# Scan of two linear-attention layers: half-width second doubling, one transpose of v, 65-column decays, and the 16x16 solve moved from VectorE to Pool

## The chip, the cores and the metric

The kernel runs on one core of one Trainium2 chip. The metric is the device time of one execution in microseconds; lower is better. A profiled execution is the source of every duration here. Engines are named as in the profile: PE (TensorE), PEld (its weight loads), DVE (VectorE), ACT (ScalarE), POOL (GpSimd), SP (SyncE, which issues most DMAs). L12 is line 12 of the kernel before.

## What is computed

The reference is a stack of a two-layer block (convolution beside a linear-attention scan, then a feed-forward net) and a second block with attention, retention and a mixture of experts. The change touches only the scan of the first block. There are 8 heads of 64 channels, two directions, 256 context tokens and 512 tokens, and two layers:

```python
decay = jnp.exp(-DECAY_SCALE * jax.nn.sigmoid(decay_b0[d] + jnp.tanh(w_lo) @ decay_up[d]))
a = jax.nn.sigmoid(iclr_b0[d] + a_lo @ iclr_up[d])
k_d = k * (1.0 + (a - 1.0) * k_a)
...
def wkv_scan(r, k, v, decay, kk, a, s0, reverse, emit):
    ...
    def step(s, inp):
        r_t, k_t, v_t, w_t, kk_t, b_t = inp          # b = kk * a
        sa = -jnp.einsum("bhvk,bhk->bhv", s, kk_t)
        s = (s * w_t[:, :, None, :] + sa[..., None] * b_t[:, :, None, :]
             + v_t[..., None] * k_t[:, :, None, :])
        y = jnp.einsum("bhvk,bhk->bhv", s, r_t) if emit else None
        return s, y
    s_fin, ys = lax.scan(step, s0, xs, reverse=reverse)
```

## The kernel before

The scan of a layer (`scan`, from L704) is done in 12 steps: four pairs of heads, and for each pair three groups of 256 tokens. A step handles one group forwards (direction 0) and one backwards (direction 1), and a group is four chunks of 64 tokens. In a chunk the recurrence becomes products of 64x64 matrices, among them the inverse of a triangular 64x64 matrix. The stages of a step s are:

- `decay` (L842): two matmuls, tanh, a running sum along each chunk (L863), one or two subtractions (L866, or L870 and L871), three exponentials (L874 to L876).
- `products` (L880): six multiplications per direction that scale k, r and kk by the decays (L887 to L894), matmuls `pg` (L906), and four masked copies of them into `GM` (L910), two per direction. Part of GM is the triangular matrix, called NT.
- `solve` (L674): NT goes to DRAM (`nsc`, L682; for direction 1 a DVE transpose `Nt`, L680, comes first). Its 64 diagonal blocks of 16x16, of both directions, four chunks and two heads, are read back with one block to a partition (`NB`, 64 partitions, one buffer; L684). There 14 rounds of a multiply (L689) and an add (L690), of 14 to 56 elements each and each needing the one before, and one write of the diagonal (L693) invert the blocks. The result goes to DRAM (`xsc`, L694).
- `solved` and `transposed` (L697, L917): four DMAs fetch the inverted blocks into 64x64 form (L702); PE transposes k, b (L925) and v (L932), and ACT copies them out.
- `inverse` (L937): two doublings, from blocks of 16 to 32 and from 32 to 64, each a DVE transpose (L948, one per direction), matmuls `py` (L954), an ACT copy, matmuls `pw` (L963) and a masked DVE copy (L967).
- `chunks` (L974): four rounds, each a chain PE, DVE (`rg`, L992), PE, ACT (L998), PE, DVE (the state M: L1009, or L1011 where there is no state yet). POOL multiplies the old state by the chunk's decay beside it (L1008), and L1009 needs that product.

While step s goes through its chunks, the inverse of step s+1 and the products and solve of step s+2 are written among them (`among`, `to_come`), with the convolution's taps (L533) and other work in the early steps. A scheduler then sets the order in each engine's queue when the program is built; at run time each engine takes its queue in that order, waiting at an instruction whose inputs are not there.

Of the kernel before, what the change touches and what calls it, by code (L numbers as in the profile page):

```python
# [28 lines left out]
CH = 64  # L29
# [22 lines left out]
def shape_constants():  # L52
    p = np.arange(128)[:, None]
    f = np.arange(128)[None, :]
    cf = {}
    cf["ident"] = (p == f).astype(np.float32)
    cf["bones"] = (p // 64 == f // 64).astype(np.float32)
    for d in range(2):
        s, t = p % 64, f % 64
        strict = (s < t) if d == 0 else (s > t)  # L60
        incl = (s <= t) if d == 0 else (s >= t)

        for i in range(2):
# [21 lines left out]

NMASK = 4 * 64
# [42 lines left out]
def tile_two_blocks(ctx: ExitStack, tc: tile.TileContext, I: dict, out: bass.AP, dump=None, stop=None):  # L129
# [508 lines left out]
    def scan_buffers(first_time, RK):  # L638
# [4 lines left out]
        for name, n, cnt in (("GM", 1024, 6), ("KR", 512, 6), ("Z", 512, 4), ("BT", 512, 4), ("XI", 256, 4), ("BK", 512, 4), ("XY", 512, 2),  # L643
                             ("Mn", 128, 4)):
# [29 lines left out]
    def solve(s, T, gs):  # L674
# [29 lines left out]
    def scan(l, S):  # L704
# [13 lines left out]
        S["rs"] = ZZ[2]  # L718
# [123 lines left out]
    def decay(q, l, S, pr, d, g):  # L842
# [9 lines left out]
        tA = wk.tile([128, 4, 256], F32, name="tA", tag="spl", bufs=4)  # L852
        tB = wk.tile([128, 4, 256], F32, name="tB", tag="spl", bufs=4)
        c4 = lambda v: v.rearrange("p (c t) -> p c t", t=CH)
        sa = tA[:, 0:2]
        for i in range(2):
            nc.scalar.activation(tA[:, i], pz[i][:, 0:256], AF.Tanh, scale=0.5,
                                 bias=HB[:, 8 * i + 4 * d + pr:8 * i + 4 * d + pr + 1])
        nc.scalar.activation(sa, sa, AF.Copy, scale=0.5, bias=0.5)
        yield  # L860
        sg, a = tA[:, 0], tA[:, 1]
        cum, oth = tA[:, 2], tA[:, 3]
        nc.vector.tensor_tensor_scan(cum, cst("scan"), sg, 0.0, op0=OP.mult, op1=OP.add)  # L863
        P, Pi, Pp, tmp = tB[:, 0], tB[:, 1], tB[:, 2], tB[:, 3]
        if d == 0:
            nc.vector.tensor_tensor(oth, cum, sg, op=OP.subtract)  # L866
            incl, excl = cum, oth
# [9 lines left out]
        q.update(ts=ts, a=a, P=P, Pi=Pi, Pp=Pp, tmp=tmp)  # L877
        yield

    def products(q, l, S, pr, d, g, KK, get, emit):  # L880

        RK = S["RK"]
        ts, a, P, Pi, Pp, tmp = (q[n] for n in ("ts", "a", "P", "Pi", "Pp", "tmp"))
# [3 lines left out]
        nc.vector.tensor_tensor(KR[:, 0], KK[:, ts], Pp, op=OP.mult)  # L887
        nc.vector.tensor_tensor(tmp, KK[:, ts], a, op=OP.mult)
        nc.vector.tensor_tensor(BK[:, :, 1], c4(tmp), c4(Pi), op=OP.mult)
        nc.scalar.activation(a, a, AF.Identity, scale=vc("k_a", 4 * l + pr), bias=KC[:, pr, 0:1])  # L890
        nc.vector.tensor_tensor(a, a, RK[:, 1, pr % 2, ts], op=OP.mult)
        nc.vector.tensor_tensor(BK[:, :, 0], c4(a), c4(Pi), op=OP.mult)
        if emit:
            nc.vector.tensor_tensor(KR[:, 1], RK[:, 0, pr % 2, ts], P, op=OP.mult)  # L894

        PC = wk.tile([128, 4], F32, name="PC", tag="pc", bufs=6)
        nc.vector.tensor_copy(PC, c4(P)[:, :, 63 if d == 0 else 0])
# [19 lines left out]
    def transposed(q, l, S, pr, d, g, KK, get, emit):  # L917

        BK, VY, t0 = q["BK"], S["VY"], GRP[g][1]
        BT = get("BT").rearrange("p (c a k) -> p c a k", c=4, a=2)  # L920
# [7 lines left out]
        Z = get("Z").rearrange("p (i c v) -> p i c v", i=2, c=4)  # L928
        pv = bank("pg", None, "pv").rearrange("p (i c v) -> p i c v", i=2, c=4)[:, 0]
        for c in range(4):  # L930
            for h in range(2):
                nc.tensor.matmul(pv[HR[h], c], lhsT=VY[HR[h], 0, pr, t0 + CH * c:t0 + CH * c + CH], rhs=ident[HR[h], HR[h]], start=True, stop=True)  # L932
        nc.scalar.activation(Z[:, 0], pv, AF.Copy)
        q.update(Z=Z, BT=BT)
        yield

    def inverse(T, gs):  # L937
# [8 lines left out]
        def first(q, d):  # L946
            a = ("X", "XI") if d == 0 or i else ("XI", "X")
# [17 lines left out]
        def merge(q, d):  # L965
            mk = CM[:, (2 * d + i) * 64:(2 * d + i + 1) * 64]
            nc.vector.copy_predicated(q["XI"], bc(mk), q["p"])  # L967

        for i in range(2):
            for f in (first, left, out_, right, merge):  # L970
                each(f)
                yield

    def chunks(l, S, pr, gs, T, state, emit, final, get):  # L974
# [4 lines left out]
        def chunk(q, d, n):  # L979
# [5 lines left out]
            for h in range(2):  # L985
                nc.tensor.matmul(pr_[HR[h], 0:64], lhsT=GM[HR[h], 0, c, 0], rhs=Z[HR[h], 0, c], start=True, stop=M is None)
# [11 lines left out]
            nc.scalar.activation(Z[:, 1, c], ps_[:, 0:64], AF.Copy)  # L998
            yield
            if not (final and n == 3):  # L1000
                pm = bank("sm", None, "psM")
                for i in range(2):
                    for h in range(2):
                        nc.tensor.matmul(pm[HR[h], 0:64], lhsT=BT[HR[h], c, i], rhs=Z[HR[h], i, c], start=i == 0, stop=i == 1)
# [8 lines left out]
            if emit:  # L1013
# [1168 lines left out]
```

## Time and profile before

| | |
|---|---|
| median of 3 runs | 4024.76 us (4021.48 to 4025.88) |
| profiled execution, its time | 4035.13 us |
| its span | 4033.3 us |
| PE / DVE / ACT / POOL busy | 94% / 68% / 42% / 8% |
| mean granted TensorE clock | 0.961 |
| scan of the first layer | about 293 to 701 us |
| scan of the second layer | about 1530 to 1895 us |

Busy times are unions of an engine's instructions. A matmul's end is modelled, so a high share of PE is not PE at its limit. Rows of a timeline give the start and the time of an instruction, or of several alike in a row; "[0.82 <-PE pg L906]" is idle time of the engine just before it and what ended it.

### The profile page before, as it was taken

The numbers are of one execution on the slowest core, as the hardware profiler recorded it, in microseconds if no ns is written. First come the engines' busy times: TensorE is split into PE (matmuls) and PEld (weight loads), VectorE is DVE, ScalarE is ACT, GpSimd is POOL, SyncE is SP. The second block draws the span as 40 slices with busy tenths as digits, with TensorE's granted clock in tenths as the row PEclk, the third lists the DMA queues.
The fourth block names the chain that finished last, engine by engine and source line by source line (L and its number), as shares of the span: only waits on it lengthen the run. The fifth ranks groups of instructions, "written<-read, shape, count | busy, mean of one in ns | idle before, by whom it ended". The sixth has DMA issues, their size and how long they took to land. (4 is left out here: it accounts for less than half of the span.)

```text
span 4033.3 us, 69782 instructions
## 1 busy us (share of the span) xinstructions
PE 3787.4 (94%) x27963; PEld 2847.6 (71%) x27963; DVE 2757.5 (68%) x5535; ACT 1707.5 (42%) x2552; POOL 330.9 (8%) x301
## 2 busy tenths in 40 slices
PE   6998999999999998899999998997999999999997
PEld 4786777788888786776787786675565777764443
DVE  4778875753433778876745455657877899987776
ACT  3234352321212334442322244544655676666565
POOL 0000111000000000110000000001101122122111
PEclk8999999999999998899999998997999999999999
DMA  6122323332422221123545421035979899998996
GB/s 206 44 79 67 113 65 95 124 126 84 126 79 90 96 71 27 32 42 107 164 138 165 108 81 42 1 117 186 348 289 347 304 360 369 369 353 327 373 370 241
DMA packets 353980, 677.87 MB, mean 168 GB/s; under 512 B 118760, under 2 KB 230195, under 8 KB 323539
## 3 DMA queue, kind: packets, MB, share of 16 engines
q1 hardware_dynamic: 343024, 636.89, 45.1%
q0 software_dynamic: 9376, 34.63, 3.4%
q8 instruction: 221, 3.62, 0.4%
q10 hardware_dynamic: 1250, 1.85, 0.1%
q14 instruction: 109, 0.89, 0.1%
HBM read 635.39 MB, written 37.90 MB: 167 GB/s over the span
## 5 line engine op out<-in xcount | busy, mean ns | idle before, releaser
L431 ACT ACTIVATE wh<-wst 128x1024 fp32r<-128x1024 f32 (+2 forms) x222 | 222.8, 1004 | 988.9 <-PE pc L441 519.9
L1795 DVE TENSOR_TENSOR ml<-E,mh 128x2048 fp32r<-128x2048 f32 x236 | 536.1, 2286 | 92.0 <-PE pu L1843 44.3
L1794 ACT ACTIVATE mh<-E 128x2048 fp32r<-128x2048 f32 x236 | 447.7, 1916 | 187.6 <-PE pu L1843 147.5
L441 PE MATMUL px<-Hh,wl 128*128 128x512 f32 (+2 forms) x1216 | 485.9, 400 | 15.6 <-DVE wl L432 15.5
L441 PE MATMUL px<-Hh,wh 128*128 128x512 f32 (+3 forms) x1216 | 485.3, 401 | 13.6 <-ACT wh L431 7.1
L441 PE MATMUL px<-Hl,wh 128*128 128x512 f32 (+3 forms) x1216 | 484.7, 399 | 1.0 <-DVE Hl L419 1.0
L432 DVE TENSOR_TENSOR wl<-wst,wh 128x1024 fp32r<-128x1024 f32 (+2 forms) x222 | 255.4, 1152 | 270.5 <-ACT wh L431 268.2
L1843 PE MATMUL pu<-ml,ch 128*64 128x512 f32 (+2 forms) x968 | 273.0, 399 | 21.1 <-DVE ml L1795 20.9
L1843 PE MATMUL pu<-mh,ch 128*128 128x512 f32 (+1 forms) x968 | 280.2, 404 | 6.9 <-DVE ch L1831 4.2
L441 PEld LDWEIGHTS px<-Hh,wl 128*128 128x128 f32 (+1 forms) x1216 | 231.0, 190 | 74.7 <-DVE wl L432 20.9
L441 PEld LDWEIGHTS px<-Hh,wh 128*128 128x128 f32 (+1 forms) x1216 | 231.4, 191 | 72.9 <-ACT wh L431 9.7
L441 PEld LDWEIGHTS px<-Hl,wh 128*128 128x128 f32 (+1 forms) x1216 | 231.2, 190 | 57.0 <-DVE Hl L419 5.0
L533 DVE SCALAR_TENSOR_TENSOR acc<-ZC,VT,acc 128x272 f32<-128x272 f32 (+2 forms) x600 | 253.6, 479 | 2.6 <-ACT acc L528 2.5
L1843 PEld LDWEIGHTS pu<-mh,ch 128*128 128x128 f32 (+1 forms) x968 | 172.4, 185 | 86.8 <-issue 25.4
L1795 DVE TENSOR_TENSOR ml<-st,mh 128x2048 fp32r<-128x2048 f32 x86 | 196.0, 2286 | 42.8 <-PE pu L1843 24.5
L1843 PEld LDWEIGHTS pu<-ml,ch 128*64 128x64 f32 (+2 forms) x968 | 149.8, 159 | 90.7 <-DVE ml L1795 32.3
L441 PE MATMUL pc<-Hh,wh 128*128 128x256 f32 x672 | 192.9, 288 | 0.9 <-ACT Hh L418 0.9
L441 PE MATMUL pc<-Hl,wh 128*128 128x256 f32 x672 | 191.7, 285 | 0.5 <-DVE Hl L419 0.5
L441 PE MATMUL pc<-Hh,wl 128*128 128x256 f32 (+1 forms) x672 | 190.4, 284 | 0.1
L1794 ACT ACTIVATE mh<-st 128x2048 fp32r<-128x2048 f32 x86 | 163.2, 1917 | 55.4 <-PE pu L1843 31.7
L315 DVE SCALAR_TENSOR_TENSOR as<-adt,CS,as 128x512 f32<-128x512 f32 x224 | 161.3, 747 | 33.8 <-DMA adt<-in_w_ada_dram 19.4
L1099 DVE SCALAR_TENSOR_TENSOR XT<-px,MOD,XT 128x512 f32<-128x512 f32 x66 | 49.5, 750 | 188.9 <-PE px L441 188.6
(596 smaller groups left out, 7949.8 us busy)
## 6 DMA issues: line engine op xcount, KB each, us to landing
E<-in_w_mlp_dram SPq DMA_DIRECT2D x288, 1024.0 KB
st<-in_w_mlp_dram SPq DMA_DIRECT2D x94, 1024.0 KB
wst<-in_w_in_dram SPq DMA_DIRECT2D x29, 1024.0 KB
adt<-in_ada_w_dram SPq DMA_DIRECT2D x96, 256.0 KB
adt<-in_w_ada_dram SPq DMA_DIRECT2D x96, 256.0 KB
wst<-in_ffn_wg_dram SPq DMA_DIRECT2D x22, 1024.0 KB
wst<-in_ffn_wu_dram SPq DMA_DIRECT2D x22, 1024.0 KB
adaw<-in_ada_w_dram SPq DMA_DIRECT2D x16, 1024.0 KB
```

What stands on the lines that cost most here:

```text
L315: nc.vector.scalar_tensor_tensor(acc[s], t, c, acc[s], op0=OP.mult, op1=OP.add)
L431: nc.scalar.activation(wh, t[:, :, c0:c0 + n], AF.Copy)
L432: nc.vector.tensor_tensor(wl, t[:, :, c0:c0 + n], f32(wh), op=OP.subtract)
L441: nc.tensor.matmul(p[0:m, 0:n], lhsT=wa[:, k, 0:m], rhs=ha[:, k, a:a + n], start=k == 0 and first, stop=k == nk - 1 and last)
L533: nc.vector.scalar_tensor_tensor(o, z[:, j + a:j + a + n], cw(j), o, op0=OP.mult, op1=OP.add)
L1099: nc.vector.scalar_tensor_tensor(o, src, gate, o, op0=OP.mult, op1=OP.add)
L1794: nc.scalar.activation(wh, t, AF.Copy)
L1795: nc.vector.tensor_tensor(wl, t, f32(wh), op=OP.subtract)
L1843: nc.tensor.matmul(p[0:xa.shape[2]], lhsT=xa[:, kt], rhs=w[part][:, c:c + 512], start=kt == 0 and j == 0, stop=last and j == len(parts) - 1)
```

## The change

Four things change in the scan.

1. The 14 rounds and the diagonal write of `solve` are issued on POOL instead of DVE. The DMAs around them stay where they were.
2. The second doubling works on the 32 columns that it needs: transposes of 32 of each 64 columns, matmuls with 32 moving columns, and a plain copy of 32 rows per head, on DVE for one head and on ACT for the other, where a masked copy of everything was.
3. v is transposed once for each pair of heads and group and kept in a ring of four buffers (`V`), not once per direction; `Z` is split into `V` and `SA`.
4. The running sum has 65 columns per chunk, the first a zero that POOL writes (two memsets of 128x4 per step), so that the inclusive and exclusive sums are two views of it: one subtraction falls away in either direction, two exponentials take the place of three, and the multiplications of k and b by the inverse decay become one of 512 columns.

```diff
-            nc.vector.tensor_tensor(t, NB[:, 0:k, k:k + 1].to_broadcast(sh), NB[:, k:k + 1, k + 1:16].to_broadcast(sh), op=OP.mult)
-            nc.vector.tensor_tensor(NB[:, 0:k, k + 1:16], NB[:, 0:k, k + 1:16], t, op=OP.add)
+            nc.gpsimd.tensor_tensor(t, NB[:, 0:k, k:k + 1].to_broadcast(sh), NB[:, k:k + 1, k + 1:16].to_broadcast(sh), op=OP.mult)
+            nc.gpsimd.tensor_tensor(NB[:, 0:k, k + 1:16], NB[:, 0:k, k + 1:16], t, op=OP.add)
...
-        nc.vector.tensor_scalar(NB.rearrange("p a b -> p (a b)")[:, 0:256:17], ones[0:64, 0:16], 1.0, None, op0=OP.mult)
+        nc.gpsimd.tensor_scalar(NB.rearrange("p a b -> p (a b)")[:, 0:256:17], ones[0:64, 0:16], 1.0, None, op0=OP.mult)
...
+        nc.gpsimd.memset(full[:, 0, :, 0:1], 0.0)
...
-        nc.vector.tensor_tensor_scan(cum, cst("scan"), sg, 0.0, op0=OP.mult, op1=OP.add)
-        P, Pi, Pp, tmp = tB[:, 0], tB[:, 1], tB[:, 2], tB[:, 3]
-        if d == 0:
-            nc.vector.tensor_tensor(oth, cum, sg, op=OP.subtract)
...
+        nc.vector.tensor_tensor_scan(tA[:, 520:780], cst("scan"), tA[:, 0:260], 0.0, op0=OP.mult, op1=OP.add)
+        if d:
+            rest = c4(tB[:, 516:776])
+            nc.vector.tensor_tensor(rest, sums[:, :, 64:65].to_broadcast([128, 4, 65]), sums, op=OP.subtract)
...
-        nc.scalar.activation(P, incl, AF.Exp, scale=-CDEC)
-        nc.scalar.activation(Pi, incl, AF.Exp, scale=CDEC)
-        nc.scalar.activation(Pp, excl, AF.Exp, scale=-CDEC)
...
+        nc.scalar.activation(E, sums, AF.Exp, scale=-CDEC)
+        nc.scalar.activation(Pi, sums[:, :, incl], AF.Exp, scale=CDEC)
...
-        nc.vector.tensor_tensor(BK[:, :, 1], c4(tmp), c4(Pi), op=OP.mult)
...
-        nc.vector.tensor_tensor(BK[:, :, 0], c4(a), c4(Pi), op=OP.mult)
...
+        nc.vector.tensor_tensor(BK.rearrange("p c a t -> p a c t"), sa,
+                                Pi[:, None].to_broadcast([128, 2, 4, CH]), op=OP.mult)
...
+        if (pr, g) not in Vs:
+            Vs[pr, g] = get("V").rearrange("p (c v) -> p c v", c=4)
...
+        def first2(q, d):
+            nc.vector.transpose(q["X"][:, :, half(d)], q["XI"][:, :, half(d)])
...
+                    nc.tensor.matmul(q["p"][HR[h], c], lhsT=q["NT"][HR[h], c], rhs=q["X"][HR[h], c, half(d)], start=True, stop=True)
...
+        def merge2(q, d):
+            for h in range(2):
+                rows = slice(64 * h + 32 * d, 64 * h + 32 * d + 32)
+                o = q["XI"][rows, :, half(1 - d)]
+                if h:
+                    nc.scalar.activation(o, q["p"][rows], AF.Copy)
+                else:
+                    nc.vector.tensor_copy(o, q["p"][rows])
```

The scheduler orders the queues anew. First place: DVE in the second layer's scan, where the masked copies into GM and the transpose `Nt` of the eighth step's solve stand beside the first transposes (of `X` and `XI`, here under the name of their buffer, XT) of the seventh step's inverse. Before:

```order
L910 TENSOR_TENSOR scanbuf_14686<-pg,CB 128x512
L992 TENSOR_SCALAR rg<-psR 128x64
L910 TENSOR_TENSOR scanbuf_14686<-pg,CB 128x512
L992 TENSOR_SCALAR rg<-psR 128x64
L910 TENSOR_TENSOR scanbuf_14686<-pg,CB 128x512 x2
L680 STREAM_TRANSPOSE Nt<-scanbuf_14686 128x256
L543 SCALAR_TENSOR_TENSOR ZC_13447<-cmean,acc 128x512
L1009 SCALAR_TENSOR_TENSOR XT<-psM,PC,XT 128x64 x2
L549 COPY CVC<-cvar 128x8
L948 STREAM_TRANSPOSE XT<-XT 128x256
```

The same place now:

```order
L1027 TENSOR_SCALAR rg<-psR 128x64
L908 TENSOR_TENSOR scanbuf_14542<-pg,CB 128x512
L1027 TENSOR_SCALAR rg<-psR 128x64
L908 TENSOR_TENSOR scanbuf_14542<-pg,CB 128x512
L948 STREAM_TRANSPOSE XT<-XT 128x256
L908 TENSOR_TENSOR scanbuf_14542<-pg,CB 128x512
L948 STREAM_TRANSPOSE XT<-XT 128x256
L908 TENSOR_TENSOR scanbuf_14542<-pg,CB 128x512
L680 STREAM_TRANSPOSE Nt<-scanbuf_14542 128x256
```

`Nt` of the next step stood ahead of the inverse's first transpose; it now stands behind it.

Second place: DVE one step on. Before, the products stand ahead of the inverse's transposes:

```order
L892 TENSOR_TENSOR XT<-tA,tB 128x4x64
L690 TENSOR_TENSOR NB<-NB,nbt 64x14
L1011 TENSOR_SCALAR XT<-psM,PC 128x64 x2
L992 TENSOR_SCALAR rg<-psR 128x64 x2
L910 TENSOR_TENSOR scanbuf_14686<-pg,CB 128x512
L338 RECIPROCAL rcn<-rcn 128x8
L910 TENSOR_TENSOR scanbuf_14686<-pg,CB 128x512 x3
L1050 TENSOR_TENSOR VY<-spread,VY 128x512
L948 STREAM_TRANSPOSE XT<-XT 128x256
L680 STREAM_TRANSPOSE Nt<-scanbuf_14686 128x256
```

Now (L887 to L892 are products, L908 the copies into GM; four more rows, then `Nt`):

```order
L948 STREAM_TRANSPOSE XT<-XT 128x256
L887 TENSOR_TENSOR tA<-zz_14544,tA 128x4x64
L888 TENSOR_TENSOR tA<-tA,RK 128x4x64
L887 TENSOR_TENSOR tA<-zz_14544,tA 128x4x64
L948 STREAM_TRANSPOSE XT<-XT 128x256
L889 TENSOR_TENSOR XT<-tA,tB 128x2x4x64
L888 TENSOR_TENSOR tA<-tA,RK 128x4x64
L892 TENSOR_TENSOR scanbuf_14543<-RK,tB 128x256
L889 TENSOR_TENSOR XT<-tA,tB 128x2x4x64
L895 COPY PC<-tB 128x4
L1046 TENSOR_SCALAR XT<-psM,PC 128x64 x2
L908 TENSOR_TENSOR scanbuf_14542<-pg,CB 128x512
```

Seven of the products have moved behind the first transpose, so that they too lie between it and `Nt`.

Third place: the end of a solve, the one of the second step of the first layer, on DVE before (other work lies between its operations), and the same solve on POOL now, with what follows it there (L1043 is the decay of the state, L1008 before).

```order
L689 TENSOR_TENSOR nbt<-NB 64x26
L690 TENSOR_TENSOR NB<-NB,nbt 64x13x2
L1009 SCALAR_TENSOR_TENSOR XT<-psM,PC,XT 128x64
L689 TENSOR_TENSOR nbt<-NB 64x14
L1009 SCALAR_TENSOR_TENSOR XT<-psM,PC,XT 128x64
L690 TENSOR_TENSOR NB<-NB,nbt 64x14
L533 SCALAR_TENSOR_TENSOR acc<-ZC_479,VT,acc 128x272 x2
L992 TENSOR_SCALAR rg<-psR 128x64 x2
L533 SCALAR_TENSOR_TENSOR acc<-ZC_479,VT,acc 128x239
```

```order
L689 TENSOR_TENSOR nbt<-NB 64x26
L690 TENSOR_TENSOR NB<-NB,nbt 64x13x2
L689 TENSOR_TENSOR nbt<-NB 64x14
L690 TENSOR_TENSOR NB<-NB,nbt 64x14
L1043 TENSOR_SCALAR XT<-XT,PC 128x64 x6
L689 TENSOR_TENSOR nbt<-NB 64x14
L693 TENSOR_SCALAR NB<-ones 64x16
```

The solve stands in POOL's queue in one piece, and the decays of the state stand behind it.

## Rows read from the trace of the kernel before

**Rows 1.** Windows of both scans: PE, PEld, DVE, ACT, POOL busy us (instructions).
```profile
293.00:701.00 408.00, 367.11 (x6915) 292.36 (x6914) 317.99 (x1141) 162.66 (x411) 43.92 (x87) 0.97 0.31 83
1530.00:1895.00 365.00, 325.15 (x6311) 265.01 (x6312) 275.80 (x1027) 156.66 (x406) 47.05 (x84) 0.92 0.20 45
```
**Rows 2.** Line L694, the DMA behind each solve: first and last start, by scan.
```profile
L694 SPq DMA_DIRECT2D xsc<-NB x12: 574/575/596, 330.9 to 661.7; - x12
...
L694 SPq DMA_DIRECT2D xsc<-NB x12: 574/574/590, 1566.8 to 1856.6; - x12
```
**Rows 3.** Groups by line, whole run: count, busy us, mean ns of one, idle before.
```profile
L690 DVE TENSOR_TENSOR NB<-NB,nbt 64x14 f32<-64x14 f32 (+6 forms) x336 | 62.7, 187 | 2.3
L689 DVE TENSOR_TENSOR nbt<-NB 64x14 f32<-64x14 f32 (+6 forms) x336 | 62.6, 186 | 8.7 <-DMA NB<-nsc 6.5
L948 DVE STREAM_TRANSPOSE XT<-XT 128x256 f32<-128x256 f32 x96 | 40.6, 432 | 7.8 <-DMA XT<-xsc 7.5
L932 PE MATMUL pv<-CF,VY 64*64 64x64 f32 x768 | 28.3, 221 | 0.2 <-issue 0.2
L954 PE MATMUL py<-XT,scanbuf 64*64 64x64 f32 x1536 | 69.0, 229 | 11.2 <-DVE XT L948 8.7 <-DMA XT<-xsc 1.8
L963 PE MATMUL pw<-XT 64*64 64x64 f32 x1536 | 62.1, 226 | 1.0 <-ACT XT L957 0.4
```
**Rows 4.** Timeline of SP around one solve of the second layer: start us, us.
```profile
1752.71 1.23 SPq L682 DMA_DIRECT2D nsc<-Nt  x2
1755.56 0.59 SPq L684 DMA_DIRECT2D NB<-nsc  x1
1767.60 0.57 SPq L694 DMA_DIRECT2D xsc<-NB  x1
1770.16 2.94 SPq L702 DMA_DIRECT2D XT<-xsc  x4
```
**Rows 5.** Timeline of DVE in the same stretch.
```profile
1749.71 0.69 DVE L910 TENSOR_TENSOR scanbuf<-pg,CB 128x512 f32<-128x512 f32 x1 [0.18 <-PE pg L906]
1750.72 0.69 DVE L910 TENSOR_TENSOR scanbuf<-pg,CB 128x512 f32<-128x512 f32 x1 [0.32 <-PE pg L906]
...
1752.28 0.40 DVE L680 STREAM_TRANSPOSE Nt<-scanbuf 128x256 f32<-128x256 f32 x1
...
1759.38 0.16 DVE L689 TENSOR_TENSOR nbt<-NB 64x14 f32<-64x14 f32 x1
...
1763.35 0.21 DVE L689 TENSOR_TENSOR nbt<-NB 64x56 f32<-64x56 f32 x1
1763.59 0.21 DVE L690 TENSOR_TENSOR NB<-NB,nbt 64x56 f32<-64x56 f32 x1
...
1773.58 0.45 DVE L948 STREAM_TRANSPOSE XT<-XT 128x256 f32<-128x256 f32 x1
```
**Rows 6.** Tile NB: ns min/median/max, first and last start us.
```profile
L689 DVE TENSOR_TENSOR nbt<-NB x336: 135/189/245, 314.7 to 1856.2; 64x14 f32<-64x14 f32 x24, 64x36 f32<-64x36 f32 x24, 64x50 f32<-64x50 f32 x24, 64x56 f32<-64x56 f32 x24
...
L684 SPq DMA_DIRECT2D NB<-nsc x24: 573/592/598, 312.0 to 1845.8; - x24
```
**Rows 7.** POOL's arithmetic: the state's decay by line, and line L1756's times.
```profile
L1008 POOL TENSOR_SCALAR XT<-XT,PC 128x64 f32<-128x64 f32 x160 | 85.0, 542 | 895.9 <-DVE XT L1011 373.9 <-DVE XT L1009 342.9 <-DVE nbt L689 92.9
...
L1756 POOL TENSOR_TENSOR hr<-hr,AS x8: 1255/1405/3039, 2752.8 to 2769.2; 128x512 f32<-128x512 f32 x8
```
**Rows 8.** Timeline of DVE, then POOL: a state and its decays.
```profile
1844.25 0.47 DVE L1009 SCALAR_TENSOR_TENSOR XT<-psM,PC,XT 128x64 f32<-128x64 f32 x2
...
1844.62 0.85 POOL L1008 TENSOR_SCALAR XT<-XT,PC 128x64 f32<-128x64 f32 x2 [11.37 <-DVE XT L1009]
```
**Rows 9.** Timeline of DVE, then POOL: a row of products beside one decay.
```profile
1690.62 0.41 DVE L887 TENSOR_TENSOR scanbuf<-zz,tB 128x256 f32<-128x256 f32 x1
...
1693.30 0.41 DVE L891 TENSOR_TENSOR tA<-tA,RK 128x256 f32<-128x256 f32 x1
...
1690.79 3.23 POOL L1008 TENSOR_SCALAR XT<-XT,PC 128x64 f32<-128x64 f32 x1 [1.11 <-DVE XT L1009]
```

More of the change, by code (lines that the diff above doesn't have):

```diff
@@ L851, in decay @@
         yield
[L852 to L855, printed above, removed]
+        tA = wk.tile([128, 1024], F32, name="tA", tag="spl", bufs=4)
+        tB = wk.tile([128, 1024], F32, name="tB", tag="spl", bufs=4)
+        c4 = lambda v: v.rearrange("p (c t) -> p c t", c=4)
+        full, sums = tA[:, 0:520].rearrange("p (i c t) -> p i c t", i=2, c=4), c4(tA[:, 520:780])
@@ L927, in transposed @@
         yield
[L928 to L934, printed above, removed]
+        if (pr, g) not in Vs:
+            Vs[pr, g] = get("V").rearrange("p (c v) -> p c v", c=4)
+            pv = bank("pg", None, "pv").rearrange("p (i c v) -> p i c v", i=2, c=4)[:, 0]
+            for c in range(4):
+                for h in range(2):
+                    nc.tensor.matmul(pv[HR[h], c], lhsT=VY[HR[h], 0, pr, t0 + CH * c:t0 + CH * c + CH], rhs=ident[HR[h], HR[h]], start=True, stop=True)
+            nc.scalar.activation(Vs[pr, g], pv, AF.Copy)
+        q.update(Z=(Vs[pr, g], SA), BT=BT)
         yield
@@ L946, in first @@
         def first(q, d):
-            a = ("X", "XI") if d == 0 or i else ("XI", "X")
+            a = ("X", "XI") if d == 0 else ("XI", "X")
             nc.vector.transpose(q[a[0]], q[a[1]])
@@ L965, in merge, with left2, out2, right2 @@
         def merge(q, d):
-            mk = CM[:, (2 * d + i) * 64:(2 * d + i + 1) * 64]
+            mk = CM[:, d * 64:(d + 1) * 64]
             nc.vector.copy_predicated(q["XI"], bc(mk), q["p"])
[L969 to L972, printed above, removed]
+        for f in (first, left, out_, right, merge):
+            each(f)
+            yield
+        half = lambda d: slice(32 * d, 32 * d + 32)
+        c32 = lambda v: v[:, 0:128].rearrange("p (c t) -> p c t", c=4)
+        def first2(q, d):
+            nc.vector.transpose(q["X"][:, :, half(d)], q["XI"][:, :, half(d)])
+        def left2(q, d):
+            q["p"] = c32(bank("iv", None, "py"))
+            for c in range(4):
+                for h in range(2):
+                    nc.tensor.matmul(q["p"][HR[h], c], lhsT=q["NT"][HR[h], c], rhs=q["X"][HR[h], c, half(d)], start=True, stop=True)
+        def out2(q, d):
+            nc.scalar.activation(q["Y"][:, :, 0:32], q["p"], AF.Copy)
+        def right2(q, d):
+            q["p"] = c32(bank("iv", None, "pw"))
+            for c in range(4):
+                for h in range(2):
+                    nc.tensor.matmul(q["p"][64 * h + 32 * d:64 * h + 32 * d + 32, c], lhsT=q["Y"][HR[h], c, 0:32], rhs=q["XI"][HR[h], c, half(1 - d)],
+                                     start=True, stop=True)
+        def merge2(q, d):
+            for h in range(2):
+                rows = slice(64 * h + 32 * d, 64 * h + 32 * d + 32)
[4 more added lines that the diff above has]
+                    nc.vector.tensor_copy(o, q["p"][rows])
+        for f in (first2, left2, out2, right2, merge2):
+            each(f)
+            yield
     def chunks(l, S, pr, gs, T, state, emit, final, get):
@@ L985, in chunk @@
             for h in range(2):
-                nc.tensor.matmul(pr_[HR[h], 0:64], lhsT=GM[HR[h], 0, c, 0], rhs=Z[HR[h], 0, c], start=True, stop=M is None)
+                nc.tensor.matmul(pr_[HR[h], 0:64], lhsT=GM[HR[h], 0, c, 0], rhs=Z[0][HR[h], c], start=True, stop=M is None)
             for h in range(2):
@@ L1003, in chunk @@
                     for h in range(2):
-                        nc.tensor.matmul(pm[HR[h], 0:64], lhsT=BT[HR[h], c, i], rhs=Z[HR[h], i, c], start=i == 0, stop=i == 1)
+                        nc.tensor.matmul(pm[HR[h], 0:64], lhsT=BT[HR[h], c, i], rhs=Z[i][HR[h], c], start=i == 0, stop=i == 1)
                 yield
@@ L1018, in chunk @@
                     for h in range(2):
-                        nc.tensor.matmul(po[HR[h], c], lhsT=Z[HR[h], i, c], rhs=GM[HR[h], i, c, 1], start=M is None and i == 0, stop=i == 1)
+                        nc.tensor.matmul(po[HR[h], c], lhsT=Z[i][HR[h], c], rhs=GM[HR[h], i, c, 1], start=M is None and i == 0, stop=i == 1)
         for n in range(4):
```

47 lines of the change are left out of this document (22 added, 25 removed).

## The prediction

> **What bounds the kernel now.** I read first the windows of the two scans, since the change touches nothing else [rows 1]. They hold 773 us of the span. DVE is busy for 318 of 408 us and 276 of 365; PE shows 90%, but with modelled ends. Next I looked for the pace. The DMA that follows each solve is issued at 330.9 for the first of twelve steps and at 661.7 for the last, in the second layer at 1566.8 and 1856.6 [rows 2]: 22 periods in 620.6 us, 28.2 us each. What fills a period? The SP and DVE timelines of one step [rows 4, 5] show a loop with two hops through DRAM:
>
> - `Nt` ends at 1752.68, and NB's read is issued at 1755.56, so 2.9 us;
> - NB's read to the first multiply takes 2.7 us where DVE is free: 312.0 to 314.7 [rows 6];
> - the solve;
> - the DMA behind it at 1767.60, the read back at 1770.16, the first transpose of the inverse at 1773.58: 6.0 us.
>
> So from `Nt` to the transpose of the same step there are 11.6 us of DMA and handover plus the solve. I use 11.5. On DVE the solve alone runs at 0.24 us per operation (1763.35 to 1763.59 [rows 5]), 7.0 us for 29; with other work between its operations it takes from 8 (1759.38 to 1767.60 here [rows 4, 5]) to 16 us (314.7 to 330.9 in the first step [rows 2, 6]). Is the loop closed, that is, does `Nt` of the next step wait for the transpose? In the order before, often not: the first two places show `Nt` ahead of the transpose, or just behind it with all products done. Transposes then found their data there: the waits of L948 for the DMA come to 7.5 us in the whole run [rows 3]. DVE's own queue, solves included, sets the period before, more than the loop does.
>
> **The change, part by part.**
>
> The solve. 29 operations per step leave DVE: 62.7 + 62.6 us [rows 3] and 24 diagonal writes of about 0.16 (an estimate, between the smallest multiply, 0.135, and the mean, 0.186 [rows 3, 6]), 129 us of DVE. On POOL the trace shows no such operation. The nearest row is the state's decay, 64 columns: two of them in 0.85 us, so 0.44 for one and 0.41 from start to start, and POOL started it some 0.09 us after the end of the first state (which takes some 0.28 of the pair's 0.47 from 1844.25, an estimate, since the two overlap; the decay starts at 1844.62) [rows 8]. The solve has 14 to 56 columns, 40 on average, but two tensor inputs, and each operation waits for the one before. I take 0.41 + 0.09 = 0.50 us, 14.5 us per solve, because that row is nearest in size. Lower bound: DVE's pace, 0.24, 7 us. Upper bound: the decay's mean with its waits, 0.542 [rows 7], and 0.09, 18.3 us.
>
> The page "GPSIMD Engine Reference" of the Trainium skill (section 3.1) gives 4497 ns for a two-input operation of 2048 columns there against 2293 on DVE, and advises against elementwise work on that engine. With the 1255 ns at 512 columns in this trace [rows 7] an estimate from that page is 0.17 us fixed and 2.1 ns a column, so 0.26 us for 40 columns; with the handover the solve would take 10 us, and the sum below would give about no change. No run here shows it.
>
> The order. The scheduler has put the transpose earlier: in the first two places it now stands ahead of `Nt` of the next step. This closes the loop. Between the first transpose and `Nt` lie, in the first place, two transposes of 0.43, two masked copies of 0.69 and `Nt`, 2.6 us; in the second seven products, four copies and more, some 9 us; where a new pair of heads begins some 15. Counted so over all 22 pairs of steps in the new order, the mean is 6.3 us. Instructions overlap by some 0.07 us each, which takes 1 us off; the four masked copies wait for PE (1749.71 and 1750.72 are 1.01 apart, against 0.69 for one [rows 5]), which adds 1.2. I take 6.5.
>
> The new period is then 6.5 + 11.5 + 14.5 = 32.5 us against 28.2, 4.3 more. Two of the 22 periods, the first of each layer, aren't ruled by it, because there the next `Nt` still stands ahead: 20 x 4.3 = 86 us. DVE's own work can't fill it: 594 us busy in both scans [rows 1] less the relief is some 430 of 773.
>
> The other edits, beside the loop. One subtraction less per direction and step, 48 of 0.41 as for a product of the same 256 columns [rows 9], 20 us of DVE; one exponential less on ACT; two multiplications of 0.41 joined into one of 512 columns, which I take at 0.69 by the masked copy [rows 5], 0.13 x 48 = 6 us. Half the transposes of v: 14 of 28.3 us of PE and half their ACT copies. The second doubling is half of 69.0 + 62.1 us of PE with half the columns: between 0 and 33 us. Its 48 transposes of 0.43 [rows 3] and as many masked copies, which I take at the same, get narrower, at most to half, up to 21 us of DVE, and 48 short copies go to ACT. None of it but the decays and products stands between a transpose and `Nt`, so I give the path 6 us for all of it, at the ends of the scans where no loop covers it. If the loop did not rule, DVE's 129 + 20 + 6 + some 15 = 170 us would count, and a good part of that would be gained.
>
> New waits. The state's decay (L1043) now stands behind a whole solve on POOL (third place). Who waits is the state's update on DVE, and behind it the next chunk. That update stands in DVE's queue near the transpose, which waits 6.0 us longer than the solve's end, so it costs nothing as long as the transpose is the later one; without that cover, up to a solve per step. The 48 memsets of four columns are bounded by 0.44 each, 21 us of POOL, behind the same solves and ahead of a running sum on DVE that has the same cover: 0. The two reloads of RK per new pair go through POOL's queue too, behind a solve: 0 to 4 us each time, at four places, 0 to 16 us, and I take 0, since products of the new pair stand behind the transpose that is later still. SP's queue keeps its DMAs; its issue of the solve's result waits for POOL in place of DVE, and what is queued behind it are the reads that need it.
>
> Sum: +86 - 6 = +80 us. The profiled execution took 4035.13 us, 10.4 over the median, so 4115 for it and 4105 on the median's scale.
>
> **The rivals.**
>
> Fast POOL. If an operation takes 0.32 us, between DVE's pace and mine, the solve is 9.3 us and the period 27.3: 20 x -0.9 - 6, about -25, and down to -70 at DVE's pace. The time would be 4000 (3955 to 4015). For it: the smallest columns are 14, and 1255 ns for 512 columns leave little fixed cost. Against: 0.41 for the nearest row, and the dependence. It decides from 0.35 us per operation downward.
>
> No change: 0.36 us, a solve of 10.5, period 28.5. With the 6 us off, 4025.
>
> POOL starved by DVE. A decay took 3.23 us, from 1690.79, while DVE ran nine products from two buffers without a gap (the first begun at 1690.62, the last at 1693.30), and ended 0.3 us after the last of them [rows 9]; the decay's mean is 0.1 over its 0.44 [rows 7, 8]. With 28 operations in a row such waits add up: at 0.3 us each 0.8 per operation, a solve of 23 us in the ten dense steps with taps and 18 in the others. That gives 10 x 12.8 + 10 x 7.8 - 6 = +200: 4225. Against: DVE idles while it waits for the transpose, and then POOL is free. I take the half of it as likely as the whole. The page "SBUF — State Buffer" of the Trainium skill (Who interferes with whom) has this as a rule: a DVE instruction with two SBUF inputs and a GpSimd instruction that reads SBUF share a read interface, and the second to come is blocked. The trace agrees, by the 3.23 us.
>
> The loop doesn't rule. If chunks or PE are later than the transpose anyway, the 170 us of DVE count by a third or so and the kernel gains 50 us: 3975. For it: PE's 90%. Against: before, the transposes hardly waited, and the solve's way through DRAM is fixed.
>
> **How the numbers follow.** Forecast (POOL at 0.42 to 0.6 us): 0.52, 4060 to 4160. Starved: 0.15, 4160 to 4225. No change: 0.08. Fast POOL: 0.17. Loop doesn't rule: 0.08. So slower by over 0.2% (8 us, about what can be told from no change here) 0.67, same 0.08, faster 0.25. The range leaves out half of the starved case and the lower part of the two fast ones: 3985 to 4190.
>
> **What would show it.** Right: the time from the first multiply to the last add on POOL at 13 to 18 us; solve-to-solve periods of 31 to 34 us; DVE idle of some 5 to 10 us per step in front of the first transpose with the DMA as releaser, where it was 7.5 us in all; DVE busy in the scans down by 150 us or more without gain. Wrong: solves on POOL under 10.5 us, periods under 28; or L948 waiting for nothing, and DVE or PE full. Starved: operations on POOL of a microsecond and more beside taps and products. The most exposed number is the 0.50 us per operation: each 0.1 us is 2.9 us per step and 58 us in all.

## The result, and the profile after

The changed kernel takes 4130.26 us (median of 4, 4120.13 to 4138.77) against 4024.61 (4021.48 to 4025.88): 1.0254 times as long, 95% interval 1.0235 to 1.0273. Between the profiled executions the span went from 4033.3 to 4118.3 us, 85 more; the one before lies 10 us above its kernel's median and the one after 10 below. The profile shows what turned up between two solves. First the scans, which now end at about 740 and 1985 us (columns as in [rows 1]):

```profile
293.00:740.00 447.00, 367.28 (x6634) 294.15 (x6634) 268.88 (x737) 154.50 (x396) 152.83 (x455) 0.90 0.27 74
1560.00:1985.00 425.00, 326.88 (x6180) 268.74 (x6179) 237.48 (x657) 151.63 (x399) 148.16 (x456) 0.88 0.17 38
```

PE's busy time is that of [rows 1] within 2 us, in stretches that are 39 and 60 us longer. DVE is busy 506 us where it was 594. The granted clock of the scans is 0.90 and 0.88, where it was 0.97 and 0.92. The DMA behind each solve, by scan (as in [rows 2]):

```profile
L694 SPq DMA_DIRECT2D xsc<-NB x12: 574/575/590, 327.3 to 704.4; - x12
...
L694 SPq DMA_DIRECT2D xsc<-NB x12: 574/574/590, 1602.7 to 1946.4; - x12
```

The 22 periods sum to 720.8 us, 32.8 each, against 28.2: 100 us more. The groups by line that answer [rows 3, 7] (L1043 is the state's decay, L908 the masked copies into GM, which waited 16.0 us before):

```profile
L948 DVE STREAM_TRANSPOSE XT<-XT 128x256 f32<-128x256 f32 x48 | 21.1, 442 | 135.2 <-DMA XT<-xsc 135.2
L908 DVE TENSOR_TENSOR scanbuf<-pg,CB 128x512 f32<-128x512 f32 x80 | 54.9, 687 | 41.5 <-PE pg L904 41.0
L954 PE MATMUL py<-XT,scanbuf 64*64 64x64 f32 x768 | 50.6, 298 | 103.7 <-DVE XT L948 103.7
L963 PE MATMUL pw<-XT 64*64 64x64 f32 x768 | 35.2, 247 | 0.3 <-ACT XT L957 0.3
L689 POOL TENSOR_TENSOR nbt<-NB 64x14 f32<-64x14 f32 (+6 forms) x336 | 108.5, 323 | 90.8 <-DMA NB<-nsc 67.6
L690 POOL TENSOR_TENSOR NB<-NB,nbt 64x14 f32<-64x14 f32 (+6 forms) x336 | 106.5, 317 | 23.6
L1043 POOL TENSOR_SCALAR XT<-XT,PC 128x64 f32<-128x64 f32 x160 | 74.1, 473 | 336.1 <-DVE XT L1044 308.0 <-DVE XT L1046 27.8
```

DVE now waits 135.2 us in front of L948 for the blocks that come back from DRAM; it waited 7.8. Behind it PE waits 103.7 us at L954 for that transpose, where it was 11.2. One period shows the whole loop. SP, POOL and DVE in the second layer (start us, us; POOL's first and last rows of a solve):

```profile
1713.04 0.57 SPq L694 DMA_DIRECT2D xsc<-NB  x1
1715.55 2.60 SPq L702 DMA_DIRECT2D XT<-xsc  x4
...
1727.82 0.59 SPq L684 DMA_DIRECT2D NB<-nsc  x1
1743.94 0.57 SPq L694 DMA_DIRECT2D xsc<-NB  x1
```
```profile
1731.14 0.21 POOL L689 TENSOR_TENSOR nbt<-NB 64x14 f32<-64x14 f32 x1
...
1743.70 0.22 POOL L690 TENSOR_TENSOR NB<-NB,nbt 64x14 f32<-64x14 f32 x1
```
```profile
1718.55 0.45 DVE L948 STREAM_TRANSPOSE XT<-XT 128x256 f32<-128x256 f32 x1 [6.32 <-DMA XT<-xsc]
...
1722.77 0.69 DVE L908 TENSOR_TENSOR scanbuf<-pg,CB 128x512 f32<-128x512 f32 x1 [1.43 <-PE pg L904]
...
1724.39 0.44 DVE L680 STREAM_TRANSPOSE Nt<-scanbuf 128x256 f32<-128x256 f32 x1
...
1750.72 0.45 DVE L948 STREAM_TRANSPOSE XT<-XT 128x256 f32<-128x256 f32 x1 [6.73 <-DMA XT<-xsc]
```

Read it round: transpose at 1718.55, `Nt` ends at 1724.83 (6.3), NB's read is issued at 1727.82 (3.0), the first multiply starts at 1731.14 (3.3), the last addition ends at 1743.92 (12.8), and the next transpose starts at 1750.72 (6.8). Each waits for the one before (the first multiply here also for two decays of the state, which POOL starts at 1730.32); 32.2 us in all.

PE's part in the stretch from the transpose to `Nt` (columns as in [rows 1]):

```profile
1713.00:1719.00 6.00, 0.00 (x0) 0.00 (x0) 0.45 (x2) 0.00 (x0) 0.92 (x5) 0.84 0.24 44
1719.00:1722.00 3.00, 2.95 (x44) 2.95 (x46) 2.34 (x7) 0.77 (x2) 0.00 (x0) 0.50 0.28 65
```

PE does nothing for 6 us while it waits for the transpose. When it starts, its granted clock is 0.50, the lower of TensorE's two levels (1.2 of 2.4 GHz), and the matmuls done at it are those of the inverse and `pg`, on which the masked copies and `Nt` wait. By the clock records of the trace, 18 of the 20 steps behind the first of each layer have such a piece between transpose and `Nt`, 4.6 us a step on the mean; in the kernel before it is one step of 20. L954's mean is 298 ns, where it was 229 [rows 3].

### The profile page after: what moved, and what is told of

It reads as the page before. It is cut to its first block, busy times and chain, and to the rows that moved or that the text cites. A ratio compares the mean times of both kernels' runs of the same rounds, so it can differ in the third digit from the quotient of the medians.

```text
span 4118.3 us, 69005 instructions
## 1 busy us (share of the span) xinstructions
PE 3776.6 (92%) x27579; PEld 2843.4 (69%) x27579; DVE 2660.8 (65%) x4743; ACT 1693.9 (41%) x2529; POOL 540.9 (13%) x1045
## 5 line engine op out<-in xcount | busy, mean ns | idle before, releaser
L441 PE MATMUL px<-Hh,wl 128*128 128x512 f32 (+2 forms) x1216 | 485.3, 399 | 14.5 <-DVE wl L432 14.5
L533 DVE SCALAR_TENSOR_TENSOR acc<-ZC,VT,acc 128x272 f32<-128x272 f32 (+2 forms) x600 | 251.0, 480 | 2.6 <-ACT acc L528 2.5
L1957 POOL DMA_INDIRECT out_dram<-XT,idx x34 | 116.7, 3433 | 513.0 <-DVE XT L1955 284.6
```

Of the source, the lines that this page charges most:

```text
L441: nc.tensor.matmul(p[0:m, 0:n], lhsT=wa[:, k, 0:m], rhs=ha[:, k, a:a + n], start=k == 0 and first, stop=k == nk - 1 and last)
L533: nc.vector.scalar_tensor_tensor(o, z[:, j + a:j + a + n], cw(j), o, op0=OP.mult, op1=OP.add)
L1957: nc.gpsimd.indirect_dma_start(out=ov, out_offset=bass.IndirectOffsetOnAxis(ap=idx[:, 0:1], axis=0), in_=y, in_offset=None, compute_op=OP.add)
```

## The experiments

**Which of the four edits.** The solve back on DVE (its multiply, its addition, shown here, and its diagonal write), the other three edits kept:

```diff
-            nc.gpsimd.tensor_tensor(NB[:, 0:k, k + 1:16], NB[:, 0:k, k + 1:16], t, op=OP.add)
+            nc.vector.tensor_tensor(NB[:, 0:k, k + 1:16], NB[:, 0:k, k + 1:16], t, op=OP.add)
```

> The changed kernel with its solve put back on DVE; the three other edits stay. The scheduler then puts Nt of the next step ahead of the transpose again in most steps. Theory (loop through the solve closed by the new order, with the solve on Pool as its cause): faster than the kernel before by 20 to 45 us (3980 to 4005), the wait of the first transposes for their DMA back under 10 us in all (135 us in the changed kernel). Rival (the other edits are at fault: memsets of Pool ahead of the running sums, ACT copies, narrow copies): slower than before by 50 us or more.

4001.82 us, ratio 0.9956 (0.9935 to 0.9977). And the reverse, the kernel before with nothing but these three instructions on POOL:

> The kernel before with its solve on Pool and nothing else. Its order, too, has the transpose ahead of Nt, with 0.7 to 1.3 us per step more between them than the changed kernel. Theory: the loop closes as in the changed kernel, periods of 33 to 34 us, 4120 to 4170, so slower than before by as much as the whole change or somewhat more. Rival (other edits at fault): within 20 us of the kernel before.

4162.3 us, ratio 1.035 (1.0324 to 1.0376). First the kernel with the solve on DVE, the DMA behind each solve by scan and the group of L948:

```profile
L694 SPq DMA_DIRECT2D xsc<-NB x12: 574/575/590, 323.5 to 649.6; - x12
...
L694 SPq DMA_DIRECT2D xsc<-NB x12: 574/575/590, 1546.2 to 1828.7; - x12
```
```profile
L948 DVE STREAM_TRANSPOSE XT<-XT 128x256 f32<-128x256 f32 x48 | 20.9, 435 | 8.7 <-DMA XT<-xsc 8.7
```

Then the same of the kernel with nothing but the solve on POOL:

```profile
L694 SPq DMA_DIRECT2D xsc<-NB x12: 574/575/581, 322.6 to 715.0; - x12
...
L694 SPq DMA_DIRECT2D xsc<-NB x12: 574/574/575, 1619.2 to 1981.9; - x12
```
```profile
L948 DVE STREAM_TRANSPOSE XT<-XT 128x256 f32<-128x256 f32 x96 | 40.5, 433 | 147.2 <-DMA XT<-xsc 146.5 <-issue 0.4
```

Periods of 29.6 and 25.7 us without the move, 35.7 and 33.0 with it alone, and the wait comes and goes with it. In how many steps is the loop closed? Of the 20 steps behind the first of each layer, `Nt` of the next step ends behind the first transpose in 10 in the kernel before, in all 20 in the changed kernel and with the move alone, and in 5 with the solve back on DVE. The solve on POOL is the whole loss; the three other edits gain 20 us where it is on DVE (4022 to 4002) and 32 where it is on POOL (4162 to 4130; 35, if each is set against the runs of the kernel before beside it). The kernel with all but the move is the fastest of the study, faster than both.

**Does the period follow the solve?** Rounds 8 to 14 left out:

```diff
-        for k in range(1, 15):
+        for k in range(1, 8):
```

> The changed kernel with rounds 1 to 7 of the solve's 14, so 14 operations on Pool in place of 28; the rest of the inversion is left out. Theory: the solve takes about 6 us in place of 11.7, and each us is one of the period in about 20 of 22 periods: -116 us, less some 25 us for a little more work between transpose and Nt in its order: 4030 to 4060, DVE's wait before the first transposes still there. Rival (Pool and DVE contend for SBUF, and the time is lost in slower instructions of DVE, not in the loop): half of the loss comes back at most, so 4070 to 4085, with the wait before the transposes little changed per step and DVE instructions shorter.

4029.93 us, ratio 1.0026 (1.0011 to 1.0041). The other way, with a second copy of the multiply:

```diff
             nc.gpsimd.tensor_tensor(t, NB[:, 0:k, k:k + 1].to_broadcast(sh), NB[:, k:k + 1, k + 1:16].to_broadcast(sh), op=OP.mult)
+            nc.gpsimd.tensor_tensor(t, NB[:, 0:k, k:k + 1].to_broadcast(sh), NB[:, k:k + 1, k + 1:16].to_broadcast(sh), op=OP.mult)
```

> The changed kernel with each multiply of the solve issued twice, 42 operations per step on Pool; results are the same. Theory: the solve grows by 14 x 0.4 = 5.6 us, 112 us over 20 periods; its order has 1.2 us less per step between transpose and Nt, so 85 to 110 us slower than the changed kernel: 4205 to 4250. If the loop does not rule the period, well under that: under 4170.

4216.37 us, ratio 1.0481 (1.0454 to 1.0508). The solve took 6.3, 11.7 and 16.8 us in the three kernels (a mean over the steps, first multiply to last addition), the period 29.0, 32.8 and 36.5. So 0.7 us of period for each microsecond of solve on both sides: the loop rules, and a part of what the solve gains is lost again by the way from the transpose to `Nt`, which got longer when the solve was cut and shorter when it was stretched.

**Is it POOL's speed or the order?** On POOL the solve is no slower than it was on DVE among other work: 11.9 and 11.6 us in the two scans, against 13.4 and 11.8. So the loss should be in what stands between transpose and `Nt`. The writing order changed, so that products and `Nt` of step s+2 are emitted ahead of the inverse of s+1:

```diff
-            if s + 1 < 12:
-                works.append(inverse_of(s + 1))
-                for _ in range(3):
-                    yield next(works[0])
             if s + 2 < 12:
                 works.append(blocks_then_decays(s + 2))
+                for _ in range(3):
+                    yield next(works[0])
+            if s + 1 < 12:
+                works.append(inverse_of(s + 1))
```

> The changed kernel, with the products and the solve of step s+2 written ahead of the inverse of step s+1 in the program. In the order that the scheduler makes of it, the work on DVE between the first transpose and the next Nt falls from 6.0 to 2.6 us a step by the same counting; the solve stays on Pool. Theory (period = that work + DMA + solve): 3.4 us less in 20 periods, 50 to 75 us faster than the changed kernel: 4055 to 4080. Rival (Pool's solve costs by contending with DVE for SBUF): within 15 us of the changed kernel.

4050.51 us, ratio 1.0078 (1.0053 to 1.0104): 80 of the 106 us are back, a little more than expected, with the solve still on POOL; `Nt` comes behind the transpose in 13 of the 20 steps. Next, `Nt` of the next step was put ahead of the first transposes at every step by a rule to the scheduler (`behind` is the `Nt` of step s+1, which is emitted first):

```diff
+            yield from inverse(Ts[s], parts(s)[2], held.get(s + 1))
...
+        with tc.issue_after(behind) if behind is not None else nullcontext():
+            each(first)
+        yield
-        for f in (first, left, out_, right, merge):
+        for f in (left, out_, right, merge):
```

> The changed kernel with the order forced: the first transposes of an inverse are queued on DVE behind Nt of the next step, everywhere. The solve stays on Pool, with all its operations. Theory: the loop is left with 0 + 6.4 + 11.7 + 6.0 = 24 us, and DVE's and PE's own work sets the period at 24 to 27 us: 3970 to 4015, faster than the kernel before, the wait before the transposes under 60 us in all (135 in the changed kernel). Rival (contention, or Pool's slowness whatever the order): over 4060.

4045.98 us, ratio 1.0066 (1.0042 to 1.009). The expectation was missed: not faster than before, and hardly better than the looser order, though `Nt` now stands ahead in all 20 steps. Its periods and its wait:

```profile
L697 SPq DMA_DIRECT2D xsc<-NB x12: 574/575/590, 324.9 to 673.1; - x12
...
L697 SPq DMA_DIRECT2D xsc<-NB x12: 574/575/590, 1574.9 to 1864.6; - x12
```
```profile
L952 DVE STREAM_TRANSPOSE XT<-XT 128x256 f32<-128x256 f32 x48 | 20.3, 433 | 65.6 <-DMA XT<-xsc 65.6
```

In the second layer the period is back at 26.3 us, that of the kernel before. In the first it is 31.7. There transposes wait for an `Nt` that is itself late, up to 32 us behind the last addition; three of the five longest waits, the longest among them, are where the next step begins a pair of heads. A run without the rule at these steps was to show whether this is what is left:

```diff
-            yield from inverse(Ts[s], parts(s)[2], held.get(s + 1))
+            yield from inverse(Ts[s], parts(s)[2], held.get(s + 1) if (s + 1) % 3 else None)
```

> The kernel after with Nt of the next step ahead of the first transposes, as in the earlier run with that order, but without that rule where the next step begins a new pair of heads (three steps per layer, whose Nt comes late because the pair's normalisation and loads come first). There the earlier run left transposes waiting 18 to 32 us behind the last addition. Theory (what that run still lost was the rule itself being too strict at these steps, not POOL): 4015 to 4035 us, first-layer periods from 31.65 to about 30, second layer unchanged at 26.3. Rival (the rest of the loss sits with POOL: sharing of SBUF, decays behind solves): 4040 to 4050 us, periods unchanged.

4051.63 us, ratio 1.0084 (1.0064 to 1.0104), first-layer period 32.1. That theory fell, and the time is about that of the rival: freed there, `Nt` goes behind the transpose again and comes 15 to 20 us after it, so one way of waiting takes the place of the other. What separates these orders (4046 to 4052) from the solve on DVE (4002) stays open. The traces offer a candidate that no run isolates: from 293 to 660 and from 1530 to 1820 us TensorE's granted clock is 0.89 and 0.88 with the forced order, and 0.95 and 0.93 with the solve on DVE.

**Is it a shared way into SBUF?** In the kernel after, POOL's operations stretch beside products on DVE. POOL, then DVE, in the second layer:

```profile
1710.43 0.73 POOL L690 TENSOR_TENSOR NB<-NB,nbt 64x44 f32<-64x44 f32 x1
...
1733.83 0.26 POOL L690 TENSOR_TENSOR NB<-NB,nbt 64x44 f32<-64x44 f32 x1
```
```profile
1710.35 0.68 DVE L889 TENSOR_TENSOR XT<-tA,tB 128x512 f32<-128x512 f32 x1
...
1734.25 0.52 DVE L1044 SCALAR_TENSOR_TENSOR XT<-psM,PC,XT 128x64 f32<-128x64 f32 x2 [0.62 <-PE psM L1039]
```

The same operation takes 0.73 us beside a product of 512 columns and 0.26 in the 0.62 us in which DVE idles ahead of 1734.25. The 672 operations, sorted by what DVE did for most of their time, say the same. Over the shortest of their shape they take 0.33 us more on the mean beside such a product (L889, 31 of them), 0.28 beside the running sum (L866, 39) and 0.12 beside the convolution's taps (L533, 69), all of which read two inputs from SBUF; but 0.01 or less where DVE is idle (163) or makes the masked copies, one input of which lies in PSUM (L908, 41). This excess sums to 1.8 us per solve. With 0.7 us of period for one of solve, an estimate is 22 x 1.8 x 0.7 = 28 us, a quarter of the loss. Memsets of 64x256 in place of the 28 operations should do without it:

```diff
-            nc.gpsimd.tensor_tensor(t, NB[:, 0:k, k:k + 1].to_broadcast(sh), NB[:, k:k + 1, k + 1:16].to_broadcast(sh), op=OP.mult)
-            nc.gpsimd.tensor_tensor(NB[:, 0:k, k + 1:16], NB[:, 0:k, k + 1:16], t, op=OP.add)
+            nc.gpsimd.memset(NB, 0.0)
+            nc.gpsimd.memset(NB, 0.0)
```

> The changed kernel with the 28 operations of each solve replaced by 28 memsets of 64x256 on Pool, each behind the one before: about the same time on Pool (28 x 0.43 = 12 us), but nothing is read from SBUF; the solve's arithmetic is left out. The scheduler takes these for long and puts Nt ahead of the transposes again, as in e6_nt_ahead. Theory (order and latency alone): like e6_nt_ahead within 15 us, 3970 to 4015. Rival (contention for SBUF reads): at least 30 us faster than e6_nt_ahead.

4018.61 us, ratio 0.999 (0.9971 to 1.0009), 27 us faster than the forced order: neither theory, which had asked for less than 15 or for 30 and more. The memsets have a mean of 0.306 us and a median of 0.305, so they are hardly stretched. But the scheduler, which plans by its own estimate of them, put `Nt` ahead of the transposes again, and the periods are 31.7 and 26.1, those of the forced order. The spans of the two profiled executions (4031.2 and 4045.1) are 14 us apart, and the periods hold 1 of these. The run doesn't settle the price of sharing in the kernel after.

**What the other edits are worth.** The half-width second doubling alone, on the kernel before (the functions are those of the change):

```diff
-        for i in range(2):
-            for f in (first, left, out_, right, merge):
-                each(f)
-                yield
+        for f in (first, left, out_, right, merge):
+            each(f)
+            yield
...
+        for f in (first2, left2, out2, right2, merge2):
+            each(f)
+            yield
```

> The kernel before with only the half-width second doubling; solve on DVE, v and decays as before. It asks which of the three other edits gave the 20 us by which the kernel after with its solve on DVE beats the kernel before. Theory (PE is the busiest engine in the scans, and this edit alone shortens matmuls on the chain): 4003 to 4013 us, more than half of the 20. Rival (the gain is DVE's queue: subtractions, exponentials and joined products): 4016 to 4026 us, no difference from before. Periods by the theory 28.7 and 25.2 us on the way from 30.07 and 26.35 to 29.64 and 25.68; by the rival as before.

4032.32 us, ratio 1.003 (1.0015 to 1.0046): a little slower, against both theories. Windows of the kernel before, then of this one:

```profile
293.00:660.00 367.00, 327.67 (x6242) 263.22 (x6242) 303.77 (x1092) 156.52 (x388) 38.76 (x75) 0.96 0.30 81
1530.00:1820.00 290.00, 253.49 (x5075) 213.07 (x5077) 233.43 (x869) 134.53 (x344) 38.44 (x64) 0.90 0.17 34
```
```profile
293.00:660.00 367.00, 326.49 (x5980) 261.70 (x5982) 286.83 (x1041) 158.06 (x392) 36.41 (x70) 0.91 0.30 78
1530.00:1820.00 290.00, 256.56 (x4897) 213.02 (x4897) 235.59 (x874) 140.45 (x359) 37.01 (x63) 0.88 0.16 32
```

The granted clock is lower in both. Does PE lose in clock what it saves in columns? Three kernels got 64 moving columns again in these matmuls, with the halved transposes and copies kept (shown is the first product; the second is changed in the same way):

```diff
-                    nc.tensor.matmul(q["p"][HR[h], c], lhsT=q["NT"][HR[h], c], rhs=q["X"][HR[h], c, half(d)], start=True, stop=True)
+                    nc.tensor.matmul(q["p"][HR[h], c], lhsT=q["NT"][HR[h], c], rhs=q["X"][HR[h], c], start=True, stop=True)
```

> The kernel before with only the half-width second doubling (4032 us, ratio 1.003, clock 0.91 and 0.88), its matmuls again with 64 moving columns, transposes and copies half as wide. Theory A: the clock returns to 0.95 and 0.90 or more, 4005 to 4022 us, since DVE keeps its relief. Theory B: 4032 to 4050 us.

4027.5 us, ratio 1.0009 (0.999 to 1.0027), clock 0.94 and 0.93 in these windows: between the two theories, and with A's clock in the second layer alone.

> The kernel of the run with Nt ahead of the transposes (4046 us), in which the matmuls of the second doubling have 64 moving columns again and not 32; the added columns are not read by anybody, and transposes and copies stay half as wide. It asks whether PE's saved columns are worth something, or whether their loss lowers the granted clock, which was 0.97 and 0.92 in the two scans of the kernel before and 0.89 and 0.88 in the kernel with Nt ahead. Theory A (the clock: with less work PE is granted less, so that the saved columns are given back in all matmuls): granted clock up by 0.02 or more in both scans, 4020 to 4040 us. Theory B (PE's columns count as work): 0 to 20 us more, 4046 to 4066 us, clock unchanged.

4038.2 us, ratio 1.004 (1.0022 to 1.0057) against 1.0066; clock 0.89 and 0.90 against 0.89 and 0.88.

> The kernel after with its solve on DVE (4002 us, clock 0.95 and 0.93), the matmuls of the second doubling with 64 moving columns. Its clock is high already. Theory A: nothing to give back, so the columns cost what they take, 4000 to 4015 us. Theory B: 4002 to 4020 us. The two part only if it gets faster by 5 us or more, which A would allow and B not.

4007.21 us, ratio 0.9963 (0.9949 to 0.9977) against 0.9956, which both theories allow. So PE's saved columns are worth nothing that can be measured: a loss of 5 and 8 us, a gain of 5, all with intervals that overlap. Where it was a loss the clock was lower in the narrow kernel, as theory A has it, but not by the 0.02 in both scans that it asked for with `Nt` ahead. That the clock is the cause is likely and not settled. The 20 us of the three edits are not the half doubling by itself; they come from the decays or from v, or from all three together, which no run tells apart.

## Why the prediction was right, and where it was not

The forecast was slower, 4105 us, by 80; the spans differ by 85, the medians by 106. The mechanism is the one predicted, and three of its signs are there: the period, DVE's wait at L948 for the DMA (5.6 us a step), and no gain from DVE's relief. Two signs missed their size: the solve took 11.9 us, not 13 to 18, and DVE's busy time in the scans fell by 87 us, not by 150. The terms were off in both directions, -2.6, +2.9, +1.1 and +0.2 us, so that the sum came so near is in part luck. Means over the 20 periods that the loop rules, from the starts and ends in the trace:

| term of the period | predicted | measured |
|---|---|---|
| first transpose to the end of `Nt` | 6.5 | 9.4 |
| `Nt` to the first multiply | 5.5 | 6.6 |
| solve on POOL | 14.5 | 11.9 |
| last addition to the transpose | 6.0 | 6.2 |
| period | 32.5 | 34.1 |

- *The solve.* The 0.50 us per operation was too much. From start to start the median is 0.36 us, the mean 0.43: 0.21 to 0.29 of operation where nothing blocks it, 0.078 to the next, and the blocked ones on top. The mean lies at the lower edge of the 0.42 to 0.6 for which the forecast stood. The decay's 0.41, taken as the nearest row, belongs to 128 partitions by 64 columns with a scalar read from a tensor; the solve's 64 by 14 to 56 are shorter. The estimate of 0.26 us for 40 columns, worked out from the page "GPSIMD Engine Reference" of the Trainium skill (section 3.1), agrees with the measured 0.21 to 0.29. By the prediction's own formula a solve of 11.9 gives a period of 29.9 and +28 us; the sign would have stood, at a third of the size.
- *Transpose to `Nt`.* 2.9 us too short, which made up for it. In the 9.4 us DVE is busy for 6.5 and idle for 2.9; the prediction had 5.3 (6.3 less 1.0 of overlap) and 1.2. So both parts were too small. The 6.3 is a mean over 22 steps, used for 20; if the other two, where `Nt` stands ahead, went in as nothing, it is 6.9 over the 20. And the 1.2 us were for masked copies that wait for PE: they came to 1.7, and waits for other results, nearly all of PE, to 1.2 that were not counted. The copies stand behind the transposes now, PE stands behind the same transposes, and what it had not done while it waited is still to do, at the lower clock shown above: L908 waits 41.5 us in the whole run, where its line in the kernel before has 16.0:

```profile
L910 DVE TENSOR_TENSOR scanbuf<-pg,CB 128x512 f32<-128x512 f32 x80 | 54.7, 684 | 16.0 <-PE pg L906 15.2
```

- *`Nt` to the first multiply.* 3.2 us to NB's read, where 2.9 were taken, and 3.4 from there to the multiply, where 2.7 were taken with DVE free. In 5 of the 20 periods the multiply follows straight on decays of the state on POOL (0.86 us for two), as in the period above, and in one on a reload of RK; in 14 it waited for the DMA alone, 3.2 us on the mean, and why that took longer stays open.
- *The base.* The 28.2 us is the mean of all 22 periods before. The 20 that the loop came to rule took 28.9 there, from transpose to transpose, so 13 of the forecast's 86 us come from too low a base.
- *Outside the periods.* -6 us was predicted. In the profiled executions the periods grew by 100 and the span by 85, so 15 came back; the runs above show some 20 for the other edits.
- *DVE's relief.* 129 us were summed for the solve; taken alone it brought DVE's busy time from 2757.5 to 2690.8, 67 us. The sum of durations counts twice what instructions share with their neighbours. All four edits took 97, not 150 or more. None of it was gained, as predicted.
- *Waits behind a solve on POOL*, counted at 0: decay and running sum made DVE wait 6.1 and 2.2 us in the whole run. Right, and for the reason given: the transpose is later still.
- *Fast POOL* was half right: the solve was no slower on POOL than among DVE's other work, and the kernel still lost. *Starved POOL*: operations of up to 2.15 us occur, but the excess is 1.8 us per solve, not the 8 that the rival asked for. The page "SBUF — State Buffer" of the Trainium skill (Who interferes with whom) has the rule that a DVE instruction with two SBUF inputs contends with a GpSimd instruction that reads SBUF; the 0.73 against 0.26 us above agree with it.
- *The order* as the cause was right and can be said in numbers: 80 to 84 of 106 us come back with the solve still on POOL, by order alone.

## What to carry to other kernels

Before moving a chain of small operations to an idle engine, ask what its queue stood between: here the move shortened the chain a little and let the scheduler place the consumer of one step ahead of the producer of the next, which closed a loop through DRAM in every step that had been open in half of them. Count such a loop in full, from the order of the changed program and with the waits, and here the lower clock of TensorE, that a stalled engine leaves behind for the next. And undo the parts of a mixed change one by one: the other three edits together were worth keeping, and the one that carried the loss hid that.

## What was not expected of the hardware

- Two-input operations on POOL with 64 partitions and 14 to 56 elements: 0.21 to 0.29 us, and 0.078 us from the end of one to the start of the next that needs it. Tile NB of the kernel after (ns min/median/max):

```profile
L689 POOL TENSOR_TENSOR nbt<-NB x336: 206/284/2152, 313.9 to 1945.5; 64x14 f32<-64x14 f32 x24, 64x36 f32<-64x36 f32 x24, 64x50 f32<-64x50 f32 x24, 64x56 f32<-64x56 f32 x24
...
L693 POOL TENSOR_SCALAR NB<-ones x24: 260/264/526, 316.0 to 1935.9; 64x16 f32<-64x16 f32 x24
```

- The sharing is felt on both sides: a product on DVE (L887) takes 440 ns on the mean with the solve on POOL and 410 with it on DVE.
- TensorE's granted clock fell in the scans from 0.97 and 0.92 to 0.90 and 0.88, when PE began to wait for the transposes, and the mean of L963's matmuls of the same shape rose from 226 to 247 ns. In the period shown the lower level sets in while PE waits and lasts into the work behind it (0.50 from 1719 to 1722 us), so it falls on the chain itself.
- Matmuls with half the moving columns hardly freed PE: in the second doubling `py` with 32 columns has a mean of 232 ns, with 64 columns 225, `pw` 203 and 223, and both together keep PE busy for 52 and 56 us (the kernels with the half doubling alone, narrow at a clock of 0.91 and 0.88, wide at 0.94 and 0.93).
